# Table products of the scan and norm-weight products: from GpSimd to VectorE

## The chip, the cores and the metric

The kernel runs on one core of one Trainium2 chip. The metric is the device time of one execution in microseconds (us). The engines are named as the profile names them: PE (TensorE), DVE (VectorE), ACT (ScalarE), POOL (GpSimd), SP (SyncE, which only issues DMAs here). Each engine works through its own instructions in the order in which they stand, and waits where an input or a buffer is not ready.

## The reference, cut to what matters

One inference step of a hybrid decoder layer for a prompt of 512 rows and 8 sample rows, model width 1024. The rows are normalised and go through one input projection, whose columns feed a state-space head group (S5) and an attention group with three branches (compressed, selected and windowed keys). Both are gated, put side by side and projected out. The change lies in two pieces of it:

```python
def rms_norm(x, w):
    xf = x.astype(jnp.float32)
    y = xf * lax.rsqrt(jnp.mean(xf * xf, axis=-1, keepdims=True) + RMS_EPS)
    return (y * w.astype(jnp.float32)).astype(x.dtype)
...
    q = rope(rms_norm(q.reshape(B, S, N_HEADS, HEAD_DIM), q_norm_w), pos)
...
    ks = rms_norm(kv[:, :, 0::2], k_norm_w[:, None, :])
...
    a_re, a_im = mag * jnp.cos(ang), mag * jnp.sin(ang)
...
    bb_re = f_re[..., None] * br - f_im[..., None] * bi
    bb_im = f_re[..., None] * bi + f_im[..., None] * br
...
    _, _, h_re, h_im = lax.associative_scan(combine, (A_re, A_im, x_re, x_im), axis=1)
    y = (jnp.einsum('gcn,bsgn->bsgc', c_re.astype(f32), h_re)
         - jnp.einsum('gcn,bsgn->bsgc', c_im.astype(f32), h_im)
         + d_skip.astype(f32).reshape(SSM_GROUPS, SSM_GROUP) * uf)
```

Queries and keys are normalised per head of 64 and multiplied by a weight (`q_norm_w`, `k_norm_w`). The complex scan runs over 512 steps for 32 groups of 16 channels with a state of 64 each. The kernel does it in blocks of 8 steps: powers 0 to 8 of the complex decay, multiplied by B and by C, give tables with which a block's inputs become its state, and states and inputs become outputs.

## The kernel before, in words

The work falls into two phases. In the first, `dense` (L909) runs the input projection: eleven chunks of weight columns are loaded, split into a high part (`whi`, a cast on ACT) and a low part (`wlo`, a difference on DVE), and multiplied in three passes per product (`mm3`, L119: lines 121 to 123). ACT copies the query banks out of PSUM scaled (`qraw`), and DVE copies the gate banks out (`sg`, L879 and L883); PE gets its PSUM banks of pool `a` (three of them) back only then. `ssm_all` (L898) runs beside it, four times over a quarter (`sq`) of the groups: `ssm_tables` (L668) makes the tables of a quarter, `ssm_run` (L736) takes them.

In `ssm_tables` the table `P_` (powers times B, real and imaginary half `Pr`, `Pi`) and the table `WY` (powers times C) are each made of two products and a sum, twice. Before the change one product of each pair is on DVE (`V`) and the other on POOL (`G`), into `pt2` and `w2_`; the sum on DVE needs both. `P_` goes to PE for transposes (L697), whose results ACT copies to `WX`. `es` and `E` are further tables, of the phase of the scan.

In `ssm_run` ACT first writes `coef` (L739), which the two scans on DVE read (`tensor_tensor_scan`, L763), so that it has to wait for the scans of the quarter before. DVE turns the scan's result into `HB` (L770); PE multiplies it with `WY` (L782) and adds the inputs times `TT` (L787) into two PSUM banks, from which ACT copies them to `ga` (L791).

`norm_rope` (L820) is called ten times, for keys and for queries, each for four tiles of 128 rows and the 8 sample rows. ACT writes the squares of the rows to `sq`; the rows are multiplied in place by the norm weight (L837, on POOL before the change); DVE reduces the squares to `rs`, POOL takes the power -0.5 of it (`rstd_of`, L168), DVE multiplies the rows by it and does the rotary part.

The second phase starts from L960: attention of the prompt, and for the sample rows a gather of cached keys (L1319, a DMA that POOL issues) with what follows it; then gating and the output projection. It isn't touched by the change.

The order is not written out by hand. A scheduler places the instructions of the whole program from its own estimate of their durations (`schedule_with_timeline_sim=True`), on each engine's list, when the program is built. So an instruction that goes to another engine can move others, on all engines. `merge` (L130) sets only the order in which the program is recorded, and `tc.issue_after` and `tc.high_priority` bind a few places.

Of the kernel before, what the change touches and what calls it, by code (L numbers as in the profile page):

```python
# [13 lines left out]
ALU = mybir.AluOpType  # L14
# [22 lines left out]
def hymba_step_kernel(  # L37
# [9 lines left out]
    G, T = nc.gpsimd, nc.tensor  # L47
# [620 lines left out]
    def ssm_tables(sq):  # L668

        gs = slice(4 * sq, 4 * sq + 4)  # L670
        P_ = pt_("P")
        Pr, Pi, pt1, pt2 = P_[:, 0:512], P_[:, 512:1024], k2("pt"), k2("pt")

        def v4(t):
            return t.rearrange("p (g s c) -> p g s c", s=8, c=16)

        def pw4(t, e0):
            return t[:, e0:e0 + 8, gs].rearrange("p e g -> p g e").unsqueeze(3).to_broadcast([128, 4, 8, 16])

        def c4(t):  # L680
            return t[:, gs].unsqueeze(2).to_broadcast([128, 4, 8, 16])

        V.tensor_tensor(v4(pt1), pw4(pwr, 1), c4(bbr), op=ALU.mult)
        G.tensor_tensor(v4(pt2), pw4(pni, 1), c4(bbi), op=ALU.mult)
        V.tensor_tensor(Pr, pt1, pt2, op=ALU.add)
        V.tensor_tensor(v4(pt1), pw4(pwr, 1), c4(bbi), op=ALU.mult)
        G.tensor_tensor(v4(pt2), pw4(pwi, 1), c4(bbr), op=ALU.mult)
        V.tensor_tensor(Pi, pt1, pt2, op=ALU.add)
        for g2 in range(2):
            sl = slice(64 * g2, 64 * g2 + 64)  # L690
            S.copy(cb[sl, 0, :, g2, :], CTr[sl, gs])
            S.copy(cb[sl, 1, :, g2, :], CNi[sl, gs])
        WX = pt_("WX")
        for a in range(2):
            p = pb("tr")
            for b in range(4):
                T.transpose(p[:, 128 * b:128 * b + 128], P_[:, 512 * a + 128 * b:512 * a + 128 * b + 128], ident)  # L697
            S.copy(WX[:, 512 * a:512 * a + 512], p)
        p = pb("tr")
        for a in range(2):  # L700
            for gp in range(4):
                T.matmul(p[32 * gp:32 * gp + 32, 0:128], cb[:, a, gp].rearrange("p a c -> p (a c)"),
                         P_[:, 512 * a + 128 * gp:512 * a + 128 * gp + 128], start=(a == 0), stop=(a == 1),
                         skip_group_check=True, tile_position=(0, 32 * gp))
        ktt = k1("ktt")
        S.copy(ktt, p[:, 0:128])
        p = pb("tr")
        T.transpose(p[:, 0:128], ktt, ident)

        ktc = k1("ktc")  # L710
        k3_ = ktc.rearrange("p (c g) -> p g c", g=8)
        S.copy(k3_, p[:, :128].rearrange("p (g c) -> p g c", c=16))
        V.tensor_tensor(k3_[96:128], k3_[96:128], Dm[96:128, 128 * sq:128 * sq + 128].rearrange("p (g c) -> p g c", c=16),
                        op=ALU.add)
        nc.sync.dma_start(scr_k[sq, 0:128, :], ktc)

        WY = pt_("WY")
        w1_, w2_ = k2("wt"), k2("wt")
        V.tensor_tensor(v4(w1_), pw4(pwr, 0), c4(CTr), op=ALU.mult)
        G.tensor_tensor(v4(w2_), pw4(pni, 0), c4(CTi), op=ALU.mult)  # L720
        V.tensor_tensor(WY[:, 0:512], w1_, w2_, op=ALU.add)
        V.tensor_tensor(v4(w1_), pw4(pni, 0), c4(CTr), op=ALU.mult)
        G.tensor_tensor(v4(w2_), pw4(pwr, 0), c4(CNi), op=ALU.mult)
        V.tensor_tensor(WY[:, 512:1024], w1_, w2_, op=ALU.add)

        E = k2("E").rearrange("p (a g k) -> p a g k", a=2, k=64)
        for a in range(2):
            S.copy(E[:, a, :, 0:32], UW[a][:, gs, 0:32])
        es = k2("es").rearrange("p (b a g k) -> p b a g k", b=2, a=2, k=32)
        for b in range(2):  # L730
            V.tensor_tensor(es[:, b], E[:, :, :, 0:32], UW[b][:, gs, 32:33].unsqueeze(1).to_broadcast([128, 2, 4, 32]), op=ALU.mult)
        V.tensor_tensor(E[:, 0, :, 32:64], es[:, 0, 0], es[:, 1, 1], op=ALU.subtract)
        V.tensor_tensor(E[:, 1, :, 32:64], es[:, 0, 1], es[:, 1, 0], op=ALU.add)
        return WX, WY, E
# [85 lines left out]
    def norm_rope(i, keys):  # L820

        n, kv_, q_ = rowset(i)
        if keys:
            src = kv_.rearrange("p (k v n) -> p k v n", v=2, n=128)[:, :, 0, :]
            hd, h, sh = src.rearrange("p k (g d) -> p k g d", g=2), 6, (n, 3, 2)
            nw_ = nw4[:n, 1:4].unsqueeze(2).to_broadcast([n, 3, 2, 64])
            e = lambda t: t.rearrange("p (k g) d -> p k g d", g=2)
            bc = lambda t: t.unsqueeze(1).unsqueeze(1).to_broadcast([n, 3, 2, 8])
        else:
            src = q_  # L830
            hd, h, sh = src.rearrange("p (h d) -> p h d", d=64), 8, (n, 8)
            nw_ = nw4[:n, 0:1].to_broadcast([n, 8, 64])
            e = lambda t: t
            bc = lambda t: t.unsqueeze(1).to_broadcast([n, 8, 8])
        sq = k3("sq", 64 * h, n)
        S.activation(sq.rearrange("p (k n) -> p k n", n=128) if keys else sq, src, AF.Square)
        G.tensor_tensor(hd, hd, nw_, op=ALU.mult)  # L837
        rs = st([n, 14], "rsq", bufs=2, tag=f"rsq{n}")[:, 0:h]
        V.tensor_reduce(rs, sq.rearrange("p (h d) -> p h d", d=64), axis=AX.X, op=ALU.add)
        o = C_ROPE + 16 * i if i < 4 else C_ROPS  # L840
        cos, sin = bc(cst[:n, o:o + 8]), bc(cst[:n, o + 8:o + 16])
        x1, x2 = hd[..., 0:8], hd[..., 8:16]
        rstd_of(rs, rs, 64, n, h)
        rb = e(rs.unsqueeze(2)) if keys else rs.unsqueeze(2)
        V.tensor_tensor(hd, hd, rb.to_broadcast([*sh, 64]), op=ALU.mult)
        ra, rb_ = k1("ra", 128, n), k1("rb", 128, n)
        r_ = [e(t[:, 8 * h * j:8 * h * j + 8 * h].rearrange("p (h d) -> p h d", d=8)) for t in (ra, rb_) for j in range(2)]
        for out, x, cs_ in zip(r_, (x1, x2, x2, x1), (cos, sin, cos, sin)):
            V.tensor_tensor(out, x, cs_, op=ALU.mult)
        V.tensor_tensor(x1, r_[0], r_[1], op=ALU.subtract)  # L850
        last["nr"] = V.tensor_tensor(x2, r_[2], r_[3], op=ALU.add)
        if not keys:
            return
        if i < 4:
            nc.sync.dma_start(kvp_rows[128 * i:128 * i + 128], kv_[:, 0:512])
            nc.sync.dma_start(winp_rows[128 * i:128 * i + 128], kv_[:, 512:768])
        else:
            nc.sync.dma_start(kv_sample[0, :, 0].rearrange("b k g d -> b (k g d)"), kvs[:, 0:512])
            nc.sync.dma_start(win_sample[0, :, 511].rearrange("b k g d -> b (k g d)"), kvs[:, 512:768])
# [887 lines left out]
```

## Time and profile before

| | us |
|---|---|
| median of 3 runs (lowest to highest) | 485.32 (484.53 to 486.43) |
| profiled execution | 485.31 |
| its span | 483.4 |
| PE busy in the span | 456.5 (94%) |
| DVE busy | 353.8 (73%) |
| ACT busy | 241.1 (50%) |
| POOL busy | 124.8 (26%), 130 instructions |

The span is the time from the first to the last instruction of the profiled execution; 1.9 us of its time lie around it. A timeline row has the start and the length of one instruction, or of several like ones (`x2`), its engine, its line, its output and inputs; behind it, in brackets, how long the engine was idle before it and what ended that. Instructions of one engine overlap a little at their ends, so what one costs in a full row is the distance from its start to the next start, which is shorter than its shown length. Line 62 (L62) and line 61 are those of a helper through which all DVE and ACT instructions are recorded, so names of outputs and inputs tell them apart. The granted clock is the share of PE's full speed that it was given.

### The profile page before, as it was taken

The numbers are of one execution on the slowest core, as the hardware profiler recorded it, in microseconds if no ns is written. First come the engines' busy times: TensorE is split into PE (matmuls) and PEld (weight loads), VectorE is DVE, ScalarE is ACT, GpSimd is POOL, SyncE is SP. The second block draws the span as 40 slices with busy tenths as digits, with TensorE's granted clock in tenths as the row PEclk, the third lists the DMA queues.
The fourth block names the chain that finished last, engine by engine and source line by source line (L and its number), as shares of the span: only waits on it lengthen the run. The fifth ranks groups of instructions, "written<-read, shape, count | busy, mean of one in ns | idle before, by whom it ended". The sixth has DMA issues, their size and how long they took to land.

```text
span 483.4 us, 10948 instructions
## 1 busy us (share of the span) xinstructions
PE 456.5 (94%) x4258; PEld 387.9 (80%) x4258; DVE 353.8 (73%) x914; ACT 241.1 (50%) x585; POOL 124.8 (26%) x130
## 2 busy tenths in 40 slices
PE   7999999889698999979999999999999899999997
PEld 4989998688697898979867866777667599899886
DVE  6978999999998974648485875868557667774332
ACT  5914755545234222656675667747565636442100
POOL 3100045489673000063244213421324010000000
PEclk8999999899899999989999999999999899999999
DMA  8776622335256182065433272337244974612211
GB/s 285 234 218 169 112 52 89 92 91 115 48 144 191 51 195 39 1 216 177 133 102 117 88 263 88 129 122 241 92 161 132 261 179 132 173 35 77 66 45 46
DMA packets 75603, 62.84 MB, mean 130 GB/s; under 512 B 29230, under 2 KB 69024, under 8 KB 75424
## 3 DMA queue, kind: packets, MB, share of 16 engines
q1 hardware_dynamic: 66176, 36.74, 27.8%
q0 software_dynamic: 4816, 17.03, 10.7%
q10 hardware_dynamic: 4560, 8.39, 5.6%
q8 instruction: 33, 0.54, 0.5%
q14 instruction: 18, 0.15, 0.1%
HBM read 55.63 MB, written 10.70 MB: 137 GB/s over the span
## 4 chain that ended last, share of the span: by engine, by line
PE 65%; DVE 19%; issue 8%; DMA 5%; ACT 2%; POOL 1%; SPq 0%; DVEq 0%; POOLq 0%; ACTq 0%
PE a L121 9%; PE a L122 9%; PE a L123 9%; PE ph L1362 8%; PE a L1252 4%; PE a L1216 4%; PE t L1243 3%; DVE wlo L62 3%; PE t L1338 3%; DVE ga L62 3%; PE c L1535 2%; DMA kvg<-in_cache_kv_dram,idx 2%; PE t L1328 2%; DVE rsq L62 1%; DMA x<-in_x_prompt_dram 1%
## 5 line engine op out<-in xcount | busy, mean ns | idle before, releaser
L121 PE MATMUL a<-hTh,whi 128*128 128x256 f32 (+1 forms) x192 | 55.6, 291 | 7.3 <-ACT qraw L61 4.4
L122 PE MATMUL a<-hTh,wlo 128*128 128x256 f32 (+1 forms) x192 | 55.4, 290 | 0.0
L1319 POOL DMA_INDIRECT kvg<-in_cache_kv_dram,idx x32 | 31.9, 998 | 89.0 <-PE c L1119 56.1
L123 PE MATMUL a<-hTl,whi 128*128 128x256 f32 (+1 forms) x192 | 53.9, 287 | 0.0
L123 PE MATMUL a<-wlo,hTh 128*128 128x256 f32 (+1 forms) x160 | 46.6, 292 | 2.3 <-DVE wlo L62 2.3
L121 PE MATMUL a<-whi,hTh 128*128 128x256 f32 (+1 forms) x160 | 46.3, 293 | 0.0
L122 PE MATMUL a<-whi,hTl 128*128 128x256 f32 (+1 forms) x160 | 46.1, 289 | 0.0
L1362 PE MATMUL ph<-XT,W1h 128*128 128x256 f32 x256 | 44.7, 298 | 0.2 <-ACT XT L61 0.2
L121 PEld LDWEIGHTS a<-hTh,whi 128*128 128x128 f32 x192 | 36.9, 192 | 8.7 <-ACT qraw L61 4.6
L61 ACT ACTIVATE P<-a,mx 128x128 f32<-128x128 f32 (+3 forms) x64 | 33.6, 533 | 13.4 <-DVE mx L61 12.1
L61 DVE TENSOR_REDUCE mx<-a 128x1 f32<-128x384 f32 (+3 forms) x48 | 28.0, 596 | 13.5 <-PE a L1217 13.4
L122 PEld LDWEIGHTS a<-hTh,wlo 128*128 128x128 f32 x192 | 36.9, 192 | 0.6 <-issue 0.4
L123 PEld LDWEIGHTS a<-hTl,whi 128*128 128x128 f32 x192 | 36.4, 192 | 0.0
L121 PE MATMUL a<-woh,mixh 128*128 128x256 f32 x128 | 36.2, 285 | 0.0
L123 PE MATMUL a<-wol,mixh 128*128 128x256 f32 x128 | 36.1, 284 | 0.0
L122 PE MATMUL a<-woh,mixl 128*128 128x256 f32 x128 | 35.8, 282 | 0.0
L1362 PEld LDWEIGHTS ph<-XT,W1h 128*128 128x128 f32 x256 | 34.8, 190 | 1.0 <-ACT XT L61 0.6
L123 PEld LDWEIGHTS a<-wlo,hTh 128*128 128x128 f32 x160 | 31.0, 194 | 2.9 <-DVE wlo L62 2.5
L1322 POOL COPY Vs<-kvg 128x256 f32<-128x256 f32 x32 | 14.5, 454 | 70.2 <-DMA kvg<-in_cache_kv_dram,idx 47.7
L121 PEld LDWEIGHTS a<-whi,hTh 128*128 128x128 f32 x160 | 30.7, 194 | 1.1 <-issue 0.6
L122 PEld LDWEIGHTS a<-whi,hTl 128*128 128x128 f32 x160 | 30.8, 193 | 0.9 <-issue 0.9
L61 ACT COPY pT<-t 128x512 f32<-128x512 f32 x40 | 22.9, 587 | 12.9 <-PE t L1243 10.1
(412 smaller groups left out, 1272.1 us busy)
## 6 DMA issues: line engine op xcount, KB each, us to landing
w<-in_w_in_dram SPq DMA_DIRECT2D x16, 512.0 KB
out_dram<-in_cache_win_dram ACTq DMA_DIRECT2D x8, 511.0 KB
x<-in_x_prompt_dram SPq DMA_DIRECT2D x4, 512.0 KB
TT<-scr_k SPq DMA_DIRECT2D x4, 512.0 KB
w<-in_w_in_dram SPq DMA_DIRECT2D x16, 128.0 KB
W1r<-in_cmp_w_dram SPq DMA_DIRECT2D x4, 512.0 KB
wk<-in_cache_win_dram SPq DMA_DIRECT2D x8, 256.0 KB
wv<-in_cache_win_dram SPq DMA_DIRECT2D x8, 256.0 KB
```

Of the source, the lines that this page charges most:

```text
L61: return f(*args, **kw)
L62: return f(*args, **kw)
L121: T.matmul(out, ah, bh, start=start, stop=False, skip_group_check=True)
L122: T.matmul(out, al, bh, start=False, stop=False, skip_group_check=True)
L123: T.matmul(out, ah, bl, start=False, stop=stop, skip_group_check=True)
L1216: T.matmul(bank, QTv(g, r)[:, qsl], KTv(g, a)[:, brs, :n], start=(a == 0), stop=False, skip_group_check=True)
L1243: T.transpose(p[:, 128 * r:128 * r + 128], P[r][:, br, 128 * kt:128 * kt + 128], ident)
L1252: mm = T.matmul(po[64 * br:64 * br + 64, :], kvt[kt - 1][:, c0:c0 + 64], behind[kt - 1][br][0], start=(kt == 1), stop=(kt == i + 1), tile_ ...
L1319: G.indirect_dma_start(out=gt_, out_offset=None, in_=ckv, in_offset=bass.IndirectOffsetOnAxis(ap=idx[:, 2 * pr_ + b2, jq:jq + 1], axis=0))
L1322: G.tensor_copy(Vs[b2][:, 2 * jq:2 * jq + 2, :], gf[:, :, 384:512])
L1338: T.transpose(p[:, 256 * g + 128 * b2:256 * g + 128 * b2 + 128], gts[jq][b2][:, o:o + 128], ident)
L1362: T.matmul(ph3[:, kd], (W1l if part == 1 else W1h)[kd][a][:, wsl], (xl if part == 2 else xh)[:, e, a:a + 256], start=(jq == 0 and kd == 0 ...
```

## The change

Four lines of `ssm_tables` and one of `norm_rope` call `V` where they called `G`. With four calls of the one and ten of the other, 26 instructions go from POOL's list to DVE's. Operands and results are the same.

```diff
--- before.py
+++ after.py
@@ -681,10 +681,10 @@
             return t[:, gs].unsqueeze(2).to_broadcast([128, 4, 8, 16])
 
         V.tensor_tensor(v4(pt1), pw4(pwr, 1), c4(bbr), op=ALU.mult)
-        G.tensor_tensor(v4(pt2), pw4(pni, 1), c4(bbi), op=ALU.mult)
+        V.tensor_tensor(v4(pt2), pw4(pni, 1), c4(bbi), op=ALU.mult)
         V.tensor_tensor(Pr, pt1, pt2, op=ALU.add)
         V.tensor_tensor(v4(pt1), pw4(pwr, 1), c4(bbi), op=ALU.mult)
-        G.tensor_tensor(v4(pt2), pw4(pwi, 1), c4(bbr), op=ALU.mult)
+        V.tensor_tensor(v4(pt2), pw4(pwi, 1), c4(bbr), op=ALU.mult)
         V.tensor_tensor(Pi, pt1, pt2, op=ALU.add)
         for g2 in range(2):
             sl = slice(64 * g2, 64 * g2 + 64)
@@ -717,10 +717,10 @@
         WY = pt_("WY")
         w1_, w2_ = k2("wt"), k2("wt")
         V.tensor_tensor(v4(w1_), pw4(pwr, 0), c4(CTr), op=ALU.mult)
-        G.tensor_tensor(v4(w2_), pw4(pni, 0), c4(CTi), op=ALU.mult)
+        V.tensor_tensor(v4(w2_), pw4(pni, 0), c4(CTi), op=ALU.mult)
         V.tensor_tensor(WY[:, 0:512], w1_, w2_, op=ALU.add)
         V.tensor_tensor(v4(w1_), pw4(pni, 0), c4(CTr), op=ALU.mult)
-        G.tensor_tensor(v4(w2_), pw4(pwr, 0), c4(CNi), op=ALU.mult)
+        V.tensor_tensor(v4(w2_), pw4(pwr, 0), c4(CNi), op=ALU.mult)
         V.tensor_tensor(WY[:, 512:1024], w1_, w2_, op=ALU.add)
 
         E = k2("E").rearrange("p (a g k) -> p a g k", a=2, k=64)
@@ -834,7 +834,7 @@
             bc = lambda t: t.unsqueeze(1).to_broadcast([n, 8, 8])
         sq = k3("sq", 64 * h, n)
         S.activation(sq.rearrange("p (k n) -> p k n", n=128) if keys else sq, src, AF.Square)
-        G.tensor_tensor(hd, hd, nw_, op=ALU.mult)
+        V.tensor_tensor(hd, hd, nw_, op=ALU.mult)
         rs = st([n, 14], "rsq", bufs=2, tag=f"rsq{n}")[:, 0:h]
         V.tensor_reduce(rs, sq.rearrange("p (h d) -> p h d", d=64), axis=AX.X, op=ALU.add)
         o = C_ROPE + 16 * i if i < 4 else C_ROPS
```

The scheduler places the program anew. On DVE, in the first phase, around the weight split wlo_1280 (`wlo` of the first query chunk; `es` and `E` belong to the second quarter's tables, `ga` and `gc` to the first quarter's scan):

```order
 L62 TENSOR_TENSOR es_919<-E_916,UW_380 128x256
 L62 TENSOR_TENSOR es_919<-E_916,UW_381 128x256
-L61 SCALAR_TENSOR_TENSOR gates_317<-a_1384,rsd_122,gb_299 128x24
-L62 TENSOR_TENSOR E_916<-es_919 128x4x32 x2
+L62 TENSOR_TENSOR wlo_1280<-w_1265,whi_1279 128x1024
 L62 TENSOR_TENSOR ktc_662<-ktc_662,Dm_487 32x8x16
+L62 TENSOR_TENSOR E_916<-es_919 128x4x32
 L62 TENSOR_TENSOR WY_907<-wt_908,wt_909 128x512
-L62 TENSOR_TENSOR wt_908<-pni_411,ssm_325 128x512
+L62 TENSOR_TENSOR E_916<-es_919 128x4x32
 L62 TENSOR_TENSOR ga_1082<-Xc_1061,E_675 128x512
```

The split now stands right behind the two `es`, and the splits of the next chunk further up too; before, wlo_1280 stood fourteen rows behind the `es`, after the scan (`ga_1082<-coef_482`).

On ACT, before, around the second `coef` (`qraw` is a query bank that ACT copies out of PSUM, `sq` a Square for `norm_rope`):

```order
L61 COPY ktc_1336<-t_1334 128x8x16
L61 ACTIVATE qraw_314<-a_1960,rsd_122 128x256
L62 ACTIVATE sq_2212<-qraw_314 128x512
L61 ACTIVATE qraw_315<-a_2011,rsd_122 128x256
L62 COPY coef_482<-ssm_325 128x4x63
L61 ACTIVATE qraw_314<-a_1960,rsd_122 128x256
L62 ACTIVATE sq_2228<-qraw_314 128x512
L62 ACTIVATE sq_2466<-qraw_315 128x512
```

On ACT, now, around the same `coef`, and with the last of those query copies ahead of it:

```order
L61 ACTIVATE qraw_315<-a_2011,rsd_122 128x256
L62 ACTIVATE sq_2466<-qraw_315 128x512
L62 COPY ssm_326<-ssm_325 64x4x16 x2
L61 COPY ktt_1332<-t_1323 128x128
L62 COPY ssm_326<-CNi_438 64x4x16 x2
L61 COPY ktc_1336<-t_1334 128x8x16
L62 CAST whi_2204<-w_2194 128x1024
L62 ACTIVATE sq_2482<-qraw_315 128x512
L61 COPY sgS_494<-a_2091 128x8
L62 COPY coef_482<-ssm_325 128x4x63
L62 CAST whi_2208<-w_2199 128x1024
```

The second `coef` has moved behind all copies of query banks, and behind the first copy of a gate bank for the sample rows (`sgS`).

On PE, before, around the output products of the last quarter's scan (`t_2284`, `t_2285`; `a_2517` and `a_2518` are banks of the third gate chunk):

```order
L123 MATMUL a_2518<-hTl_115,whi_2208 128x264
L121 MATMUL a_2517<-hTh_111,whi_2208 128x256
L122 MATMUL a_2517<-hTh_111,wlo_2209 128x256
L123 MATMUL a_2517<-hTl_115,whi_2208 128x256
L782 MATMUL t_2284<-HB_2278,WY_1843 64x72 x2
L782 MATMUL t_2285<-HB_2278,WY_1843 64x72 x2
L782 MATMUL t_2284<-HB_2278,WY_1843 64x72 x2
```

On PE, now, at the same products (`a_2673` is the last bank of the fourth and last gate chunk):

```order
L123 MATMUL a_2673<-hTl_115,whi_2462 128x264
L121 MATMUL a_2673<-hTh_111,whi_2462 128x264
L122 MATMUL a_2673<-hTh_111,wlo_2463 128x264
L123 MATMUL a_2673<-hTl_115,whi_2462 128x264
L782 MATMUL t_2284<-HB_2278,WY_1843 64x72 x2
L782 MATMUL t_2285<-HB_2278,WY_1843 64x72 x2
L782 MATMUL t_2284<-HB_2278,WY_1843 64x72 x2
```

These products moved from among the third gate chunk's matmuls to behind the last matmul of the gates.

## Rows read from the trace of the kernel before

**Rows 1.** Busy by stretch: us, per engine busy (instructions), granted clock, DMA share, GB/s.

```profile
84.00:156.00 72.00, 60.20 (x686) 55.70 (x685) 68.94 (x131) 31.86 (x73) 48.08 (x29) 0.95 0.44 114
156.00:204.00 48.00, 45.33 (x549) 43.57 (x549) 34.03 (x111) 16.02 (x42) 0.00 (x0) 1.00 0.32 73
204.00:483.40 279.40, 269.95 (x2352) 217.32 (x2346) 177.73 (x444) 146.12 (x368) 59.98 (x80) 0.99 0.43 133
```

**Rows 2.** Waits of PE, 84 to 204 us: waiter, releaser, us in total, times, longest.

```profile
PE a L121 <- ACT qraw L61: 4.4, 1, 4.4
PE a L121 <- DVE sg L61: 2.9, 3, 1.4
PE a L123 <- DVE wlo L62: 2.3, 1, 2.3
...
PE t L697 <- ACT ga L61: 1.8, 1, 1.8
PE t L782 <- DVE HB L62: 0.7, 1, 0.7
```

**Rows 3.** Timeline of ACT: start, us, instruction, idle before and releaser.

```profile
129.24 0.40 ACT L62 COPY coef<-ssm 128x252 f32<-128x252 f32 x1 [9.11 <-DVE ga L62]
...
129.54 0.47 ACT L61 ACTIVATE qraw<-a,rsd 128x256 f32<-128x256 f32 x1
```

**Rows 4.** Timeline of POOL, the first gather.

```profile
205.55 1.13 POOL L1319 DMA_INDIRECT kvg<-in_cache_kv_dram,idx  x1 [55.08 <-PE c L1119]
```

**Rows 5.** Timeline of DVE, quiet and beside products on POOL.

```profile
74.21 0.67 DVE L62 TENSOR_TENSOR WY<-wt,wt 128x512 f32<-128x512 f32 x1
...
74.81 0.67 DVE L62 TENSOR_TENSOR P<-pt,pt 128x512 f32<-128x512 f32 x1
...
83.81 1.61 DVE L62 TENSOR_TENSOR ga<-Xc,E 128x512 f32<-128x512 f32 x1
...
86.54 1.59 DVE L62 TENSOR_TENSOR WY<-wt,wt 128x512 f32<-128x512 f32 x1
```

**Rows 6.** Timeline of POOL, 83 to 88 us.

```profile
83.31 1.56 POOL L723 TENSOR_TENSOR wt<-ssm,CNi 128x512 f32<-128x512 f32 x1 [3.82 <-DVE WY L62]
...
86.19 1.40 POOL L684 TENSOR_TENSOR pt<-pni,ssm 128x512 f32<-128x512 f32 x1 [1.33 <-DVE gc L62]
```

**Rows 7.** Timeline of DVE, first and last of 24 stretched instructions.

```profile
65.04 1.75 DVE L62 TENSOR_TENSOR es<-E,UW 128x256 f32<-128x256 f32 x2 [0.76 <-ACT E L62]
...
150.22 0.79 DVE L62 TENSOR_TENSOR ga<-Xc,E 128x512 f32<-128x512 f32 x1 [1.70 <-DMA out_dram<-kvt]
```

**Rows 8.** Timeline of DVE, rows with POOL idle or out of the way.

```profile
80.57 0.75 DVE L62 TENSOR_TENSOR es<-E,UW 128x256 f32<-128x256 f32 x2
...
91.58 1.19 DVE L62 TENSOR_TENSOR wlo<-w,whi 128x1024 fp32r<-128x1024 f32 x1
...
112.70 0.54 DVE L62 TENSOR_TENSOR kvt<-kvt,rsq 128x384 f32<-128x384 f32 x1
...
113.17 0.15 DVE L62 TENSOR_SCALAR rsq<-rsq 8x8 f32<-8x8 f32 x1
```

**Rows 9.** Timeline of POOL, a power that stands alone.

```profile
140.12 2.48 POOL L168 TENSOR_TENSOR rsq<-rsq,mhalf 128x8 f32<-128x8 f32 x1 [0.84 <-DVE rsq L62]
```

**Rows 10.** Timeline of DVE under that power.

```profile
139.89 1.21 DVE L62 TENSOR_TENSOR wlo<-w,whi 128x1024 fp32r<-128x1024 f32 x1
```

**Rows 11.** Timeline of POOL, products that waited for ACT's Square.

```profile
94.03 1.94 POOL L837 TENSOR_TENSOR kvs<-kvs,nw 8x384 f32<-8x384 f32 x1 [4.44 <-ACT sq L62]
...
130.75 5.49 POOL L837 TENSOR_TENSOR qraw<-qraw,nw 128x512 f32<-128x512 f32 x2 [2.68 <-ACT sq L62]
```

**Rows 12.** Timeline of PE, last matmul of bank a_2091 and of the gates.

```profile
141.38 0.28 PE L123 MATMUL a<-hTl,whi 128*128 128x264 f32 x1
...
197.73 0.28 PE L123 MATMUL a<-hTl,whi 128*128 128x264 f32 x1
```

**Rows 13.** Timeline of DVE, evacuation of a_2091.

```profile
146.04 0.42 DVE L61 TENSOR_TENSOR sg<-a,rsT 128x256 f32<-128x256 f32 x1
```

## The prediction

> **What bounds the kernel now.** I read the busy shares first (PE 94%, DVE 73%), then the 40 slices, where DVE is full in a third of the span, then busy time by stretch, the waits of PE there, and the timelines of DVE, POOL and ACT. Over the whole span this is a TensorE kernel, but not where the change lies. From 84 to 156 us DVE is busy 68.94 of 72.00 us and PE only 60.20, with the clock granted to PE at 0.95; from 156 to 204 us PE is at 45.33 of 48.00 and DVE has room; after 204 us PE is the bound again, 269.95 of 279.40 [rows 1]. So in the first phase PE waits for VectorE, and PE's own list says for what: 4.4 us for an ACT copy of a q bank, 2.9 for the gate evacuations on DVE, 2.3 for a weight split (wlo), 1.8 for an ACT copy of the scan's output, 0.7 for HB [rows 2]. The ACT copies are late for VectorE too: ACT stood 9.11 us ahead of `coef`, which waited for a scan on DVE, and the q copy that PE needed came right behind it, at 129.54 [rows 3]. The phase ends when the gather of the cached keys starts, at 205.55 [rows 4].
>
> **What a product on GpSimd costs now.** In a quiet stretch VectorE does a 128x512 sum or product every 0.60 us (74.21 to 74.81, each shown as 0.67 long). Beside a GpSimd product it does not: those at 83.81 and 86.54 took 1.61 and 1.59 [rows 5], and they meet the two GpSimd products there, 83.31 to 84.87 and 86.19 to 87.59 [rows 6]. The excess is 0.92 each. I went through DVE's timeline from 62.6 to 150.5 us and took from each instruction's start-to-start time that of its own shape in quiet stretches: 24 instructions are over by more than 0.15, the first in the two `es` at 65.04 (1.75 for two, quiet 0.75 as at 80.57), the last a `ga` at 150.22; together 19.4 us [rows 7, 8]. Every one of the 24 meets a moved product. A power does nothing of the kind: under the one at 140.12, 2.48 long, a 1024-column split took 1.21, against 1.19 for one with POOL idle [rows 8 to 10].
>
> The Trainium skill says of this (SBUF — State Buffer, "Who interferes with whom") that a VectorE instruction with two SBUF inputs contends with a GpSimd instruction that reads SBUF, and that whichever issues first keeps the shared ports for its whole length. By that rule VectorE would lose up to the whole 1.56 and 1.40 us at the two places, an estimate of 26 x 1.48 = 38.5 us for all products, and the time would go to the low end below. The trace shows the exclusion, but 0.92 of it.
>
> **The change part by part.** It takes 26 products from POOL: four lines in each of four calls of `ssm_tables`, and one line in each of ten calls of `norm_rope`. Ten powers of `rsq` stay on POOL in this phase.
> - Added on DVE: 16 table products of 128x512 and 5 norm products of 512 columns at 0.60 us, and 5 norm products of 384 columns at 0.47 (112.70 to 113.17 [rows 8]): 12.6 + 2.35 = 14.95 us.
> - Removed on DVE: the 19.4 us of stretching. Net -4.4 us, on an engine that is full from 84 to 156 us.
> - The powers stay. Their cost on DVE is nothing by [rows 9, 10]; the other end is 0.92 each, 9.2 us. I take nothing, since the power that stands alone has no excess over it, and keep 9.2 for a rival.
> - The norm product is done in place, after ACT's Square of the same rows. POOL waited for that: 4.44 us ahead of `kvs` and 2.68 ahead of `qraw` [rows 11]. On DVE the same wait would hold all that is queued behind: scans, tables, weight splits, and PE behind these. Its cost is between 0 and 7.1 us; I take 0, because in the new order each of the ten products stands behind other VectorE work, and ACT has more idle than busy time there (31.86 of 72.00 [rows 1]) to be done with the Square first. That work hides it; if it is gone, the 7.1 is paid.
> - Moved: the scheduler sets another order. On DVE the split wlo_1280 now comes right behind the two `es` of the next table (ended at 81.3 before) and not behind the scan. Up to there DVE has 7 added products (4.2 us) and loses 4.5 of the 19.4 us, so the split ends near 82.2, if its cast on ACT, which moves up too, is there; it ended at 92.8, and PE asked for it at 92.8 - 2.3 = 90.5. The 2.3 us go. On ACT the second `coef` moves from ahead of the last q copies to behind all of them, so the 4.4 us go. The 1.8 us (the scan's output in its bank) and the 0.7 us (HB) go with a VectorE that is not stretched. Sum 9.2 us; at the other end these waits only shrink by the 4.4 us of DVE.
> - The clock: 0.95 over 72 us against 1.00 behind it [rows 1] is 72 x 0.047 = 3.4 us of full-speed work lost (0.953 before rounding), in the stretch with the two longest waits. With them I let it come back whole; at the other end nothing of it does.
> - What is late next: the gate matmuls get their banks back from DVE. Adding up quiet start-to-start times over the 125 rows of the new order from the first `pt` (62.59) to the evacuation of a_2091 gives 126.3 us for its end, where it started at 146.04 before [rows 13]. PE ended that bank at 141.7 [rows 12]; without the 9.2 us of waits and the slow clock that is 129.1, or earlier, as the second scan's output products now stand behind it. The two arrive within some 3 us of each other, so these waits, 2.9 us now, stay, and a mismatch adds 0 to 3 us; I take 1.5.
>
> The sum: -9.2 - 3.4 + 1.5 = -11.1 us. Of the 14.5 us that PE idles from 84 to 204 (11.80 + 2.67 [rows 1]) about 7 stay. Past 204 us the order differs in a few rows only and the same work follows, so the gain stays to the end. The profiled execution took 485.31 us (span 483.4 and 1.9 around it) and the median of the runs shown is 485.32, so nothing has to be corrected: 485.3 - 11.1 = 474.2 us.
>
> **The rivals.**
> 1. Only VectorE's own 4.4 us come out, because the first phase ends when DVE does and the new order merely moves PE's waits: 485.3 - 4.4 = 480.9. For it: DVE is full to 156 us. Against: from 156 to 204 us DVE has 14 us of room [rows 1], and PE ends the phase.
> 2. No change, about 485. The gain is given back at the end of the phase: in the new order the output products of the last scan stand behind all gate matmuls, no longer among them, and if HB is late there PE stands still. It decides when DVE reaches HB 11 us after PE could use it. Against: the quiet times of the new order add up to 169.8 us for that HB, and PE ended the gates at 198.0 [rows 12], so it comes there near 187.
> 3. Slower, by the norm products: the whole 7.1 us of waits for ACT's Square land on DVE, which is full, with everything behind them, and the reordering brings nothing: 485.3 - 4.4 + 7.1 = 488.0. It decides from 4.4 us of such waits on. For it: POOL did wait there. Against: the products stand later on DVE than they did on POOL.
> 4. The powers take over the collisions: ten of 0.92, 485.3 - 4.4 + 9.2 = 490.1. Against it are [rows 9, 10]. The rule of the Trainium skill's page SBUF — State Buffer above would make it so, as a power reads two inputs from SBUF.
>
> Another page of the Trainium skill, Perfetto Trace Analysis ("Optimizing Scalar/DVE Operations"), holds that with VectorE saturated it may pay to hand work to GpSimd, and adds that the two share a port, so it might not help. By its first half the change costs its 14.95 us and the time would be about 500; by [rows 5, 6] it is the second half that holds here.
>
> **How the numbers follow.** I call a change under 0.5% (2.4 us) none; that is about what a measurement of this kernel can tell. The forecast, 7 to 18 us faster: 0.66. Rival 1: 0.16. Rival 2: 0.08. Rivals 3 and 4: 0.06 and 0.04. So faster 0.82, same 0.08, slower 0.10. The low end is all of PE's idle time and lost clock in the phase gone, 14.5 + 3.4 = 17.9: 467.4. The high end is rival 1, 480.9; rivals 2 to 4, 18 in 100, lie past it.
>
> **What the profile of the changed kernel would show.** No 128x512 product on VectorE over about 0.8 us in this phase, `pt` and `wt` products there in twice the number, POOL with ten powers and nothing else. PE's waits for wlo and for the q copy gone, its clock at 1.00 from 84 to the gather, its idle time there about 7 us. The first gather at about 194.5, and from it to the end the same 278 us as now. I am wrong in the first term if stretched rows remain under the powers, in the second if PE's idle time in the phase is still over 10 us, in the last if the time behind the first gather grows.

## The result and the profile after

The changed kernel took 467.57 us (median of four runs, 465.36 to 470.97) beside 484.92 for the kernel before on the same chip: a ratio of 0.9655, 95% interval 0.9616 to 0.9694. Six more runs of it later gave 469.44 beside 484.63, 0.9683 (0.9645 to 0.9722). That is 15 to 17 us faster, where 11.1 had been forecast. The direction is right and the time lies in the forecast range, but at its edge: the low end, 467.4, stood for a phase in which TensorE neither idles nor loses any clock. The gain was put too small. The profiled execution took 465.36 us, with a span of 463.5.

The view by windows of the profile after, with the same columns as [rows 1]:

```profile
84.00:156.00 72.00, 71.53 (x831) 68.56 (x829) 68.40 (x158) 33.60 (x81) 28.66 (x10) 1.00 0.49 133
156.00:204.00 48.00, 43.16 (x626) 40.57 (x625) 39.41 (x129) 27.10 (x78) 11.50 (x14) 0.96 0.41 114
204.00:463.50 259.50, 252.36 (x2127) 201.91 (x2126) 166.93 (x418) 132.09 (x326) 48.75 (x67) 1.00 0.43 130
```

Read the first row against the first of [rows 1]. VectorE is as busy as before (68.40 of 72 us, 68.94 before), but TensorE went from 60.20 to 71.53 and its granted clock from 0.95 to 1.00. An unchanged busy share of VectorE hides that its instructions are now short: 158 in the stretch, where there were 131. The second row has less of TensorE than before only because the phase now ends inside it: the first gather starts at 188.00 (timeline of POOL), 17.55 us earlier than in [rows 4].

```profile
188.00 1.09 POOL L1319 DMA_INDIRECT kvg<-in_cache_kv_dram,idx  x1 [37.75 <-DVE ks L62]
```

What TensorE waited for from 60 to 204 us, the answer to [rows 2]:

```profile
PE t L1328 <- DMA kvg<-in_cache_kv_dram,idx: 3.6, 2, 2.8
PE a L995 <- DVE qs L62: 1.1, 1, 1.1
PE a L121 <- DVE sg L61: 0.5, 1, 0.5
PE c L1276 <- DVE KN L61: 0.2, 1, 0.2
```

The q copy (4.4), wlo (2.3), the scan's output (1.8) and HB (0.7) are gone from the list, and of the gate banks' 2.9 us 0.5 are left. The 3.6 us for the gathered rows come after the gather and are not part of the phase.

VectorE's table rows, to be read beside [rows 5] (start, us, instruction):

```profile
61.58 0.68 DVE L62 TENSOR_TENSOR pt<-ssm,ssm 128x512 f32<-128x512 f32 x1
...
62.70 0.69 DVE L62 TENSOR_TENSOR pt<-pni,ssm 128x512 f32<-128x512 f32 x1
63.31 0.69 DVE L62 TENSOR_TENSOR wt<-ssm 128x512 f32<-128x512 f32 x1
63.91 0.69 DVE L62 TENSOR_TENSOR wt<-pni,ssm 128x512 f32<-128x512 f32 x1
64.52 0.69 DVE L62 TENSOR_TENSOR P<-pt,pt 128x512 f32<-128x512 f32 x1
65.12 0.76 DVE L62 TENSOR_TENSOR es<-E,UW 128x256 f32<-128x256 f32 x2
```

One every 0.60 us, and the two `es` take 0.76 together, where [rows 7] had 1.75. The count that gave 24 stretched instructions and 19.4 us before finds none over 0.15 us from 60 to 160 us, and 1.3 us in all.

To compare all the runs I split the time from 60 us to the first gather: TensorE's idle time (length less busy time), the full-speed work lost to the clock (length times one less the granted clock), and what is left. I summed these over stretches of 2 us from the view by windows. The third term varies by 4 us, the first two together by 30, so they set when the gather comes. The column on VectorE is its busy time in the same stretch: its own work and what GpSimd adds to it.

| kernel | time, us | ratio to before | first gather | PE idle, 60 us to gather | clock lost | rest | gather to end | VectorE busy, 60 us to gather |
|---|---|---|---|---|---|---|---|---|
| before | 484.9 | 1 | 205.5 | 14.5 | 3.4 | 127.6 | 277.9 | 127.4 |
| changed | 467.6 | 0.9655 | 188.0 | 1.7 | 0.0 | 126.3 | 275.5 | 121.5 |
| changed, again | 469.4 | 0.9683 | 190.2 | 1.9 | 1.7 | 126.6 | 275.0 | 122.5 |
| e1 only tables moved | 482.4 | 0.9976 | 204.7 | 10.9 | 8.5 | 125.3 | 275.2 | 128.2 |
| e2 only norms moved | 476.6 | 0.9871 | 198.2 | 9.5 | 3.4 | 125.3 | 275.4 | 125.6 |
| e3 tables twice, late | 478.5 | 0.9889 | 200.4 | 11.2 | 5.1 | 124.1 | 276.7 | 135.3 |
| e4 no products | 469.7 | 0.9704 | 191.9 | 3.8 | 3.4 | 124.7 | 277.7 | 108.8 |
| e5 tables twice, early | 481.4 | 0.9925 | 203.8 | 10.7 | 5.1 | 128.1 | 275.0 | 134.8 |
| e6 copies for e5's products | 473.5 | 0.9765 | 197.6 | 4.5 | 6.8 | 126.2 | 275.5 | 127.1 |
| e9 norms twice | 480.9 | 0.9935 | 200.8 | 10.0 | 5.1 | 125.8 | 276.2 | 129.6 |
| e12 both twice | 491.1 | 1.0124 | 215.5 | 17.9 | 13.6 | 123.9 | 275.2 | 141.4 |
| e8 later sums on VectorE | 474.2 | 0.9780 | 192.1 | 1.7 | 5.1 | 125.3 | 280.3 | 122.3 |
| e10 idle matmuls | 470.5 | 0.9703 | 189.7 | 0.8 | 1.7 | 127.2 | 278.8 | 122.1 |
| e11 no powers | 469.1 | 0.9676 | 191.5 | 1.9 | 5.1 | 124.5 | 277.3 | 122.8 |

The clock lost is that of one execution. It differs between executions of one program: the changed kernel's mean granted clock was 0.996, 0.982, 0.982 and 0.996 in its first four runs. The idle time is the same to 0.2 us in the two profiled executions of it.

### The profile page after: what moved, and what is told of

Its sections match the earlier page's. It is cut to its first block, busy times and chain, and to the rows that moved or that the text cites. A ratio compares the mean times of both kernels' runs of the same rounds, so it can differ in the third digit from the quotient of the medians.

```text
span 463.5 us, 10940 instructions
## 1 busy us (share of the span) xinstructions
PE 449.1 (97%) x4258; PEld 382.8 (83%) x4258; DVE 348.4 (75%) x940; ACT 240.9 (52%) x585; POOL 94.7 (20%) x104
## 4 chain that ended last, share of the span: by engine, by line
PE 71%; DVE 14%; DMA 8%; POOL 3%; issue 2%; ACT 2%; SPq 0%; DVEq 0%; POOLq 0%; ACTq 0%
PE a L121 11%; PE a L122 11%; PE a L123 10%; PE ph L1362 8%; DMA kvg<-in_cache_kv_dram,idx 4%; PE a L1216 3%; PE a L1252 3%; PE t L1243 3%; POOL rsq L168 3%; PE c L1535 3%; PE t L1338 2%; DVE ga L62 2%; PE t L1328 2%; PE ph L473 1%; DMA x<-in_x_prompt_dram 1%
## 5 line engine op out<-in xcount | busy, mean ns | idle before, releaser
L121 PE MATMUL a<-hTh,whi 128*128 128x256 f32 (+1 forms) x192 | 54.6, 285 | 0.5 <-DVE sg L61 0.5
L168 POOL TENSOR_TENSOR rsq<-rsq,mhalf 128x6 f32<-128x6 f32 (+3 forms) x10 | 28.7, 2871 | 101.2 <-DVE rsq L62 101.2
L121 PE MATMUL a<-whi,hTh 128*128 128x256 f32 (+1 forms) x160 | 45.2, 287 | 0.0
L123 PE MATMUL a<-wlo,hTh 128*128 128x256 f32 (+1 forms) x160 | 45.2, 284 | 0.0
L61 ACT ACTIVATE P<-a,mx 128x128 f32<-128x128 f32 (+3 forms) x64 | 33.6, 534 | 13.6 <-DVE mx L61 12.4
L62 ACT CAST whi<-w 128x1024 fp32r<-128x1024 f32 (+4 forms) x26 | 23.9, 927 | 15.9 <-PE a L122 10.6
```

The lines of the kernel that those rows point to most:

```text
L61: return f(*args, **kw)
L62: return f(*args, **kw)
L121: T.matmul(out, ah, bh, start=start, stop=False, skip_group_check=True)
L123: T.matmul(out, ah, bl, start=False, stop=stop, skip_group_check=True)
L168: return G.tensor_tensor(out, out, mhalf[:parts, :cols], op=ALU.pow)
```

## The experiments

My theory, A: a product on GpSimd and VectorE's work exclude each other, VectorE is full, and TensorE waits behind it. The rivals were B, that the gain is the new order which the scheduler wrote, and E, that VectorE's amount of work still sets the end of the phase.

**e1 and e2: one half of the change each.**

```
e1   -        G.tensor_tensor(v4(pt2), pw4(pni, 1), c4(bbi), op=ALU.mult)
     +        V.tensor_tensor(v4(pt2), pw4(pni, 1), c4(bbi), op=ALU.mult)
     (and so L687, L720, L723; L837 stays on G)
e2   -        G.tensor_tensor(hd, hd, nw_, op=ALU.mult)
     +        V.tensor_tensor(hd, hd, nw_, op=ALU.mult)
     (the four table lines stay on G)
```

> Only the 16 table products (L684, L687, L720, L723) go to VectorE; the ten norm products (L837) stay on GpSimd. A (each product on GpSimd holds VectorE up by about 0.92 us, and VectorE's delay starves TensorE): 16 of the 26 products go, so about 16/26 of the whole change's -17.4 us, 474 us (472 to 477), with no VectorE instruction stretched beside table products. B (the gain came from the new order that the scheduler wrote, not from the engine): no such share, anything from 467 to 485. C (the gain comes from the norm products alone, since GpSimd waits for ScalarE's squares in them): 483 to 486.

> Only the ten norm products (L837) go to VectorE; the table products stay on GpSimd. A: about 10/26 of -17.4 us, 478 us (476 to 481), and the gains of this run and of the one with the tables alone add up to the whole's within 3 us. B (order): they need not add up. C (norms alone carry it): 467 to 470.

Measured: 482.43 us, ratio 0.9976 (0.9938 to 1.0013), and 476.59, 0.9871 (0.9798 to 0.9944). The halves bring 1 us, which the interval cannot tell from none, and 7, and the whole 15 to 17, so C fell too: the norms alone don't carry it. A's sizes missed for e1, by 8 us, and just met e2's range; the parts do not add up. What A says of VectorE held: ten stretched rows with some 10 us beside the ten norm products left on GpSimd in e1, 19 rows with 13.6 us in e2 (sixteen table products), and none in the whole. But neither half relieves VectorE much: a product that moves adds its own 0.5 to 0.6 us, and those that stay on GpSimd cost more each (0.75 us on the mean before, 0.85 in e2, about 1.0 in e1). From 60 us to the gather VectorE is busy 128.2 us in e1 and 125.6 in e2, where it had 127.4 before and has 121.5 in the whole. TensorE idles 10.9 and 9.5 us ahead of the gather. In e1 the wait that costs most is again an ACT copy:

```profile
PE a L121 <- ACT sgS L61: 4.1, 1, 4.1
PE t L708 <- ACT ktt L61: 2.5, 1, 2.5
PE a L1002 <- DVE sg L61: 2.2, 1, 2.2
```

Both kernels also got orders of their own, so these two runs leave B open. That e2 gains 7 us with 2 us less on VectorE speaks for some of it.

**e3: the tables a second time on GpSimd, read by nobody.**

```
         V.tensor_tensor(v4(pt2), pw4(pni, 1), c4(bbi), op=ALU.mult)
+        G.tensor_tensor(v4(dum), pw4(pni, 1), c4(bbi), op=ALU.mult)
   (and so for the other three lines)
```

> The changed kernel, and each of its 16 table products computed a second time on GpSimd into a tile that nothing reads; the order on the other engines is that of the changed kernel almost to the row, so no result is waited for. A: 16 x 0.92 = 14.7 us more of VectorE in a stretch where it has about 4 us free; 478 us (474 to 482), with some 16 VectorE instructions stretched by about 0.9 us each. B (the order made the gain, GpSimd's work beside it costs nothing): 467 to 469.

Measured: 478.46 us, 0.9889 (0.9816 to 0.9962). As A said, though not where I meant it: the scheduler put the 16 products at 144 to 169 us. Stretching there made HB late, and TensorE waited 6.0 us for it.

**e5: the same early, in halves, and the order of the other engines unchanged.** A smaller result tile let the scheduler put the products where the kernel before has them. Every row of PE, DVE and ACT stands where it stands in the changed kernel.

```
+    dum = st([128, 256], "dum", BF16)
+    def dummies(pw, e0, c):
+        for h in range(2):
+            g_ = slice(2 * h, 2 * h + 2)
+            G.tensor_tensor(dum..., pw[:, g_], c[:, g_], op=ALU.mult)
```

> The changed kernel, and each table product computed a second time on GpSimd, in two halves of 256 columns with a bf16 result that nothing reads, where the kernel before has them (from 60 us on); every row of the order on the other engines is that of the changed kernel. A (a two-operand product on GpSimd and VectorE's work exclude each other): 32 halves at half of 0.92 us, 15 us of stretching on VectorE between 60 and 110 us, time 478 us (474 to 483). B (the order made the gain): 467 to 469.

Measured: 481.40 us, 0.9925 (0.9887 to 0.9963). B as it was put is refuted: with the changed kernel's very order, and no one waiting for GpSimd, products beside VectorE's work cost 12 to 14 us. That is not yet their share of the gain. VectorE does the 26 products here as well, so from 60 us to the gather it is busy 134.8 us, 7.3 more than in the kernel before, and yet the time stays below that kernel's (484.1 beside it). The order must be worth something too; e6 says how much. The timelines of VectorE and of POOL show the exclusion row by row (start, us, instruction):

```profile
63.14 0.69 DVE L62 TENSOR_TENSOR pt<-pni,ssm 128x512 f32<-128x512 f32 x1
63.75 1.14 DVE L62 TENSOR_TENSOR wt<-ssm 128x512 f32<-128x512 f32 x1
64.81 1.13 DVE L62 TENSOR_TENSOR wt<-pni,ssm 128x512 f32<-128x512 f32 x1
65.87 1.15 DVE L62 TENSOR_TENSOR P<-pt,pt 128x512 f32<-128x512 f32 x1
66.93 1.66 DVE L62 TENSOR_TENSOR es<-E,UW 128x256 f32<-128x256 f32 x2
```

```profile
63.19 2.20 POOL L673 TENSOR_TENSOR dum<-pni,ssm 128x256 bf16<-128x256 f32 x2 [42.85 <-DVE pni L62]
65.47 2.05 POOL L673 TENSOR_TENSOR dum<-ssm,ssm 128x256 bf16<-128x256 f32 x2
67.60 1.50 POOL L673 TENSOR_TENSOR dum<-pni,ssm 128x256 bf16<-128x256 f32 x2
```

The two engines go in step. `wt` and `P` start 1.06 us apart, where the changed kernel has 0.60 for the same instructions, and a half of 0.97 to 1.14 us on GpSimd fits into each step. VectorE pays 0.45 us per half of 256 columns (28 rows, some 12 us in all; 15 were expected), almost whatever its own length: each `es` of 256 columns pays as much as a `wt` of 512. Twice 0.45 is near the 0.92 that the prediction took from [rows 5, 6] for a product of 512 columns. GpSimd is held up as well: a product of the same size with no VectorE work beside it takes 0.72 us (e9), and one of 512 columns, almost alone, 1.11 (the kernel before):

```profile
127.62 0.72 POOL L842 TENSOR_TENSOR dum<-sq,nw 128x256 bf16<-128x256 f32 x1
```

```profile
149.36 1.11 POOL L723 TENSOR_TENSOR wt<-ssm,CNi 128x512 f32<-128x512 f32 x1
```

The Trainium skill (SBUF — State Buffer, "Who interferes with whom") calls the shared ports an exclusive lock that whoever issues first has for its whole instruction, which it says beside VectorE's two-port modes. By that a half would cost 0.72 us and a product of 512 columns 1.11, estimates from these two rows; the measured 0.45 and 0.92 decide, so the rule names the right pair and a price that is too high. The prediction's estimate of 38.5 us came out higher still, because its 1.48 us a product were lengths beside a busy VectorE.

**e6: copies of one operand in the place of these products.**

```
-            G.tensor_tensor(dum..., pw[:, g_], c[:, g_], op=ALU.mult)
+            G.tensor_copy(dum..., pw[:, g_])
```

> As the run with the early halves, but each of the 32 is a copy with one operand in SBUF (256 columns of one of the product's two operands, bf16 result) instead of a product of two. If only two-operand instructions on GpSimd exclude VectorE: no stretched rows, 467 to 469. If any of its SBUF traffic does: half to all of the cost of the products, 472 to 480.

Measured: 473.51 us, 0.9765 (0.9717 to 0.9812), between the two expectations: neither free nor as dear as the products. VectorE's rows are longer by 0.20 us, each by the same:

```profile
63.72 0.69 DVE L62 TENSOR_TENSOR pt<-pni,ssm 128x512 f32<-128x512 f32 x1
64.33 0.88 DVE L62 TENSOR_TENSOR wt<-ssm 128x512 f32<-128x512 f32 x1
65.14 0.88 DVE L62 TENSOR_TENSOR wt<-pni,ssm 128x512 f32<-128x512 f32 x1
65.94 0.88 DVE L62 TENSOR_TENSOR P<-pt,pt 128x512 f32<-128x512 f32 x1
```

So one operand holds VectorE for 0.20 us and two for 0.45. TensorE's idle time grew by 2.8 us; the rest of the 4 to 6 us that it lost goes with the clock (6.8 us lost in the profiled execution).

This run also tells what the order is worth. It has the changed kernel's order (two rows of VectorE change places), no one waits for the copies, and from 60 us to the gather VectorE is busy 127.1 us, as long as in the kernel before (127.4). Yet it takes 473.5 us, and the kernel before 484.1 beside it. So of the 15 to 17 us, 4 to 6 are VectorE's relief, and the 10 or so that stay with VectorE as loaded as before come with the new order. TensorE's waits from 60 us to the gather agree:

```profile
PE t L706 <- ACT ga L61: 2.4, 1, 2.4
PE a L1006 <- DVE qs L62: 1.2, 1, 1.2
PE a L121 <- DVE sg L61: 0.9, 1, 0.9
```

The waits of [rows 2] for the q copy (4.4) and for wlo (2.3) do not come back with the load. The split is a remainder and not a measurement of its own: the stretched rows lie at 64 to 90 us here and at 65 to 151 before, and no run has the old order without GpSimd's products.

**e9 and e12: the norm products twice, and both kinds twice.** In e9 a product of the norm's size follows each square; e12 adds the halves of e5 to that.

```
         V.tensor_tensor(hd, hd, nw_, op=ALU.mult)
+        for c0, c1 in ((0, 256), (256, 64 * h)):
+            G.tensor_tensor(dum..., sq[:, c0:c1], w_..., op=ALU.mult)
```

> The changed kernel, and on GpSimd after each of the ten squares a product of the same size as the norm's (in halves of up to 256 columns, bf16 result that nothing reads). The order moves a little. A (what the norm products on GpSimd cost is the exclusion): 10 x 0.92 = 9 us on VectorE, 475 us (472 to 480). W (what they cost is that VectorE waits for them behind the powers in GpSimd's queue): nobody waits for these, 467 to 470.

> The changed kernel with both kinds of second products on GpSimd, the 32 halves of table products and the 20 halves after the squares: the load that GpSimd had before, and nobody waits for it. If the costs of the two add (9.8 and 6.8 us of length at full clock by the two runs with one kind each): 484 to 488 us, TensorE idle ahead of the first gather for 17 us. If one kind is already enough to make TensorE wait and the second finds it waiting: 480 to 484 us, idle 11 to 14 us.

Measured: e9 480.88 us, 0.9935 (0.9898 to 0.9971); e12 491.05, 1.0124 (1.0074 to 1.0174). In e9 the second products cost 11 to 13 us, 0.9 us past the end of A's range and 11 past W's. But this does not decide between A and W, because someone does wait for these products. A later Square writes the tile `sq` that they read, so ACT stood 7.45 us until GpSimd had read it, behind two powers (118.17 to 124.48 us), and the copy that TensorE needed came right behind:

```profile
128.37 0.63 ACT L62 ACTIVATE sq<-qraw 128x512 f32<-128x512 f32 x1 [7.45 <-POOL dum L842]
128.91 0.25 ACT L61 COPY ktt<-t 128x128 f32<-128x128 f32 x1
```

```profile
PE t L708 <- ACT ktt L61: 6.6, 1, 6.6
```

That one wait is 6.6 of TensorE's 10.0 us of idle time. The exclusion is there too (15 stretched rows, 7 us), but what the norm products cost by it alone stays open. e12 has the same wait of ACT (9.7 us), so it is no proof either that the costs add, though its idle time is what the sum foretold (17.9 for 17). Its time is 3 us over the forecast with 13.6 us of clock lost. VectorE is busy 141.4 us there, 14 more than in the kernel before, and e12 is slower than that kernel by 7 us.

**e4: the products left out.**

```
-        V.tensor_tensor(v4(pt2), pw4(pni, 1), c4(bbi), op=ALU.mult)   (all 26)
-        V.tensor_tensor(Pr, pt1, pt2, op=ALU.add)
+        V.tensor_tensor(Pr, pt1, pt1, op=ALU.add)
```

> The changed kernel with the 26 products left out altogether (the sums take the first product twice, the norm weight is not applied), so VectorE has some 15 us less and GpSimd only the powers. D (TensorE bounds the first phase of the changed kernel, 71.5 us busy of the 72 from 84 to 156 us): 464 to 467. E (VectorE still bounds it, 68.4 of the same 72 us): 453 to 459, the 15 us less what it has free.

Measured: 469.68 us, 0.9704 (0.9629 to 0.9778), as slow as the changed kernel and 2.7 us past D's range. With 15 us less on VectorE nothing is gained, so E is refuted. D's reason fits the changed kernel, where TensorE is busy 71.53 of the 72 us. Here, in an order of its own, TensorE is busy 68.35 of them and idles 3.8 us ahead of the gather (2.3 for gate banks, 1.4 for a q copy), so less work on VectorE doesn't remove every wait.

**e11: no powers.**

```
+        if n == 64:
+            return V.tensor_tensor(out, out, mhalf[:parts, :cols], op=ALU.mult)
         return G.tensor_tensor(out, out, mhalf[:parts, :cols], op=ALU.pow)
```

> The changed kernel with the ten powers of the head norms left out (a product of the same few columns on VectorE in their place, so the values are wrong), and so nothing on GpSimd in the first phase. If the powers take over the collisions: VectorE's work grows shorter by up to 10 x 0.92 us and the time falls by 3 us or more, 464 or less. If a power of 6 or 8 columns costs VectorE next to nothing and only runs longer itself (2.9 us): within 1.5 us of the changed kernel.

Measured: 469.05 us, 0.9676 (0.9648 to 0.9703), beside 469.44 for the changed kernel. The idle time ahead of the gather is 1.9 us with and without powers. In the changed kernel they cost nothing that shows, though the order moved here as well.

**The changed kernel again, and idle matmuls against the clock.**

```
+            if i == 0 and g == 0:
+                fill(p, 4)
+            if i == 2 and g == 1:
+                fill(p, 10)
```

> The changed kernel once more, beside the two below, to see how much of its spread (465.4 to 471.0 us in four runs) is TensorE's clock. If the clock is the spread: span times mean granted clock is the same within 1 us in all runs, 459 to 462 us, and the time follows the clock; 467 us (465 to 471).

> The changed kernel with idle matmuls of 512 bf16 columns, whose results are overwritten, where TensorE waits around the first gather: 4 ahead of the first transposes L995 (a wait of 1.1 us near 178 us) and 10 near 190 us (2.8 us for the first gathered rows). If the spells at half clock that follow these two waits come from the waits: clock 0.993 or more in every run, 464 us (462 to 466), and less spread. If they come from elsewhere: the changed kernel's time and clock, 466 to 470.

Measured: the changed kernel 469.44 us; span times clock is 458.3 to 462.6 us in its ten runs, against 1 us expected, and the times 465.4 to 471.6. Most of the spread goes with the clock, not all. With idle matmuls 470.54 us, 0.9703 (0.9672 to 0.9735): no gain. They closed the waits (0.75 us of idle left ahead of the gather), and the clock lost over the span fell from 8.4 to 5.4 us (medians of six), but the length at full clock grew by about 4 us. Why it grew I didn't find out.

**e8: the later sums on VectorE too,** as a possible better version.

```
-            G.tensor_tensor(ov, ov, tt[:, :, 0, :], op=ALU.add)
+            V.tensor_tensor(ov, ov, tt[:, :, 0, :], op=ALU.add)   (and L1192)
```

> The changed kernel with the 16 sums L1191 and L1192 of 256 columns on VectorE too (on GpSimd 0.85 us each, 13.7 us in all, in the part behind the first gather, where TensorE is 98% busy and VectorE about 70%). A (TensorE bounds that part, as it now bounds the first): within 1.5 us of the changed kernel, 466 to 469. If GpSimd's sums hold VectorE and ScalarE up (ScalarE waits 2.9 us for them): 463 to 466.

Measured: 474.17 us, 0.9780 (0.9735 to 0.9825), slower than the changed kernel by 5 to 6 us; both expectations missed. Up to the gather it idles 1.7 us as that does, and 5.1 us of clock went there. From the gather to the end it took 280.3 us, not 275: TensorE idles 14.0 us there and not 10.7. At L1252 it waits 1.8 us for ACT's copies `pT` (0.4 in the changed kernel), and 2.8 for ACT's cast `wgh` (1.6). No version that I ran beats the changed kernel.

That clock shows how thin the edge is. Here is the changed kernel, then e8, by windows (columns as above):

```profile
174.00:178.00 4.00, 2.99 (x91) 2.77 (x80) 3.92 (x16) 3.58 (x10) 0.00 (x0) 1.00 0.40 85
178.00:182.00 4.00, 3.74 (x54) 3.38 (x54) 3.48 (x16) 3.57 (x13) 0.00 (x0) 1.00 0.48 91
182.00:186.00 4.00, 4.00 (x62) 3.71 (x60) 3.57 (x17) 4.00 (x16) 0.00 (x0) 1.00 0.23 53
```

```profile
174.00:178.00 4.00, 3.47 (x98) 3.11 (x97) 3.92 (x18) 3.57 (x9) 0.00 (x0) 1.00 0.43 90
178.00:182.00 4.00, 3.34 (x23) 2.91 (x23) 2.62 (x7) 3.23 (x10) 0.00 (x0) 0.60 0.45 86
182.00:186.00 4.00, 4.00 (x41) 3.64 (x41) 2.42 (x16) 2.59 (x9) 0.00 (x0) 0.50 0.26 61
```

The same wait of about 1.1 us for `qs`, near 178 us, stands in both. In one execution the clock stayed at its upper level, in the other it fell to 0.50, the lower of its two levels (1.2 of 2.4 GHz), and 5.1 us of work were lost.

## Why the prediction was right, and where its size was off

- **VectorE, -4.4 us net: right.** The 0.60 us per added product is in the rows (0.68 to 0.69 long, 0.60 apart), and 19.4 us of stretching fell to 1.3. e5 shows that the stretching is the exclusion: with nothing else changed, 28 rows are stretched again where the halves stand. By e6 these 4.4 us are worth 4 to 6 us of time.
- **The powers at nothing: right for this kernel** (e11), and rival 4 fell with it. It is no rule: the last section shows a power in e1 that did hold VectorE up.
- **The norm products hold VectorE up for ACT's Square: 0 taken.** The rows do not show otherwise: VectorE is busy 68.40 of 72 us, and TensorE has no wait that leads there. Rival 3 did not come.
- **TensorE's waits, 9.2 us: right.** All four are gone from the list above. The sum put 6.7 of them, the q copy and wlo, down to the new order, and e6 bears that out: they stay gone with VectorE as loaded as before. The larger part of the gain is the order's.
- **The clock, 3.4 us: right in the profiled execution,** where nothing is lost ahead of the gather. That was luck in part. In the second profiled one 1.7 us are lost there, and over the whole span the six later runs lose 8.4 us to the clock (median), the kernel before beside them 9.2. On the average about 1 us of clock came back, and nearly the whole gain is length at full clock.
- **What is late next, the gate banks, +1.5 us: wrong, and this is the term that made the sum too small.** The step said that the two arrive within some 3 us of each other, so "these waits, 2.9 us now, stay, and a mismatch adds 0 to 3 us". VectorE's side was right: the first gate evacuation, which started at 146.04 before [rows 13] and was worked out to end at 126.3, starts at 127.2. But TensorE then waited 0.5 us in all for the gate banks. Two sides that come at the same time leave the wait near nothing; I had kept the old wait, which belonged to a late VectorE. That is 2.9 + 1.5 - 0.5 = 3.9 us.
- **About 7 us of idle time stay: wrong, 1.7 stayed.** Besides the 3.9, 1.9 us of waits for ACT's copies of WX were left out of the terms that go, and they went; a new wait of 1.1 us for `qs` came. So the idle time fell by 12.7 us and not by 7.7. The wait for WX is a line of the list of [rows 2] that isn't shown there:

```profile
PE t L702 <- ACT WX L61: 1.9, 2, 1.1
```

- **The same 278 us behind the gather: near.** It was 275.5 (277.9 before), with 1.7 us of clock lost there and not 4.1; that is the execution's clock more than the change. "Wrong if it grows" did not come.
- **Rival 1** (only VectorE's 4.4 us come out) was wrong: the new order did more than move waits. It names VectorE's part about rightly (4 to 6 us by e6) and leaves out the order's. **Rival 2** decides when HB is late at the end: the last HB started at 172.8 us, and TensorE didn't wait for one.

From one profiled execution to the other the first gather moved by 17.55 us: 12.7 of idle time, 3.4 of clock, 1.4 of the rest.

What stays open is why the order for the whole is so much better than those for the halves. e1 and e2 keep 10.9 and 9.5 of 14.5 us of idle time; the whole keeps 1.7. VectorE's load explains little of that, as neither half changes it by more than 2 us, and each half has an order of its own. Which rows of the order make the difference, beyond the q copy and wlo, no run shows.

## What to carry to other kernels

Before handing work to GpSimd, compare the excess that it puts on VectorE's rows beside it with what the same work would cost on VectorE: here 0.92 us against 0.60 for 512 columns (0.75 against 0.58 on the mean of all 26), so the hand-over cost more than it saved. Where a scheduler places the program anew, a move changes the order as well; to tell the two apart, keep the new order and put the old load back, as e6 does. And see that nobody waits for such a load, which e9 missed. Read the start-to-start times of a full engine and not its busy share, which here hardly moved (68.94 to 68.40 us) while TensorE won 11 us. When a stretch becomes bound by another engine, work out each remaining wait anew from when both sides arrive, and don't carry the old one over.

## What the hardware showed that I had not expected

The exclusion has a second side. Ten powers of 6 and 8 columns ran 17.3 us in all before and 28.7 after, 1.74 and 2.87 each; I read that as the powers being held up by a VectorE that is full of short instructions. The group of the changed kernel (busy us, mean ns, idle before), then the longest power and VectorE's rows beside it:

```profile
L168 POOL TENSOR_TENSOR rsq<-rsq,mhalf 128x6 f32<-128x6 f32 (+3 forms) x10 | 28.7, 2871 | 101.2 <-DVE rsq L62 101.2
```

```profile
100.69 6.05 POOL L168 TENSOR_TENSOR rsq<-rsq,mhalf 128x6 f32<-128x6 f32 x1 [2.73 <-DVE rsq L62]
```

```profile
100.53 1.21 DVE L62 TENSOR_TENSOR wlo<-w,whi 128x1024 fp32r<-128x1024 f32 x1
...
104.40 0.67 DVE L62 TENSOR_TENSOR P<-pt,pt 128x512 f32<-128x512 f32 x1
105.00 0.54 DVE L62 TENSOR_TENSOR kvt<-kvt,nw 128x384 f32<-128x384 f32 x1
106.78 0.56 DVE L62 TENSOR_TENSOR kvt<-kvt,rsq 128x384 f32<-128x384 f32 x1 [1.24 <-POOL rsq L168]
```

VectorE has no pause from 100.53 to 105.54; the power ends at 106.74, 1.2 us after VectorE ran out of work, and VectorE's next row waits 1.24 us for it. The rows at 101 to 105 have their usual lengths, so the power got in only when VectorE stood still, as I read it. Not every power waits like that: those at 108.17 and 110.72 took 1.57 and 1.62 with VectorE just as full, and what lets one in isn't shown. It costs little here, as VectorE waited 3.3 us in all for the powers.

A power that is held up can also hold VectorE. In e1 a row of 6 columns took 0.97 us, where such a row takes 0.15 elsewhere, and GpSimd had nothing but this power:

```profile
105.62 0.97 DVE L62 TENSOR_SCALAR rsq<-rsq 128x6 f32<-128x6 f32 x1
```

```profile
101.71 5.19 POOL L168 TENSOR_TENSOR rsq<-rsq,mhalf 128x6 f32<-128x6 f32 x1
```

The row at 99.91 there (0.53 us) is another such. The prediction's reading, that a power does nothing of the kind, rests on one power beside one instruction.
